# Keys and values of four attention heads as seven half-size products, in a two-layer hybrid decoder

## The chip, the cores and the metric

The program runs on one core of a Trainium2 chip. Its time is that of the device for one execution, in microseconds (us); where several runs are compared, their median stands. A core has five engines that take their own instructions in order and wait for each other by semaphores: TensorE (PE; its weight loads are listed as PEld), VectorE (DVE), ScalarE (ACT), GpSimd (POOL) and SyncE (SP). SP and POOL issue most of the DMA transfers.

## The reference

```python
DEPTH, SEQ, D_MODEL = 2, 512, 1024
def reference(x, ...):
    ...
    for l in range(DEPTH):
        x = x + 0.5 * swiglu(rms_norm(x, ffn1_norm[l]), ffn1_w_in[l], ffn1_w_out[l])
        h = rms_norm(x, mix_norm[l]) @ w_mix_in[l]
        (c_x, c_b, c_c, h_q, h_f, h_i, h_g, f_q, f_k, f_v, f_f) = jnp.split(h, split_at, axis=-1)
        y = jnp.concatenate([
            short_conv_mixer(c_x, c_b, c_c, conv_w[l]),
            hgrn2_mixer(h_q, h_f, h_i, h_g, lower_bounds[l], hgrn_out_gain[l]),
            fox_mixer(f_q, f_k, f_v, f_f, fox_f_bias[l], fox_q_gain[l], fox_k_gain[l]),
        ], axis=-1)
        x = x + y @ w_mix_out[l]
        x = x + 0.5 * swiglu(rms_norm(x, ffn2_norm[l]), ffn2_w_in[l], ffn2_w_out[l])
    return x
```

All of it is float32. The part called the mix has three token mixers side by side: a short convolution (256 channels), HGRN2, a gated linear recurrence in chunks of 64 tokens (4 heads of 64), and FoX, a forgetting attention (8 heads of 64, with normalised queries and keys). One matrix `w_mix_in` of 1024 rows makes the inputs of all three; f_q, f_k and f_v are 512 of its columns each.

## The kernel before

x stands transposed in SBUF, 1024 features in eight tiles of 128 by 512 tokens, times the gain of its norm, and as a pair of a rounded high part and the low rest. A float32 product is made of three matmuls: high by high, high by low, low by high (`mm3`, in the trace lines 328, 336 and 337).

Weights come in granules. `granule` (line 297) lets SP load a block into a buffer `st`, of which there are two; ScalarE casts it to its high part (line 314) and VectorE subtracts that from it for the low part (line 315), into a buffer `hl`, of which there are three. So a granule needs SP, then ScalarE, then VectorE before TensorE may use all of it.

The feed-forward networks on both sides of the mix already make their products in seven half-size products instead of eight (`plan`, `halved`, lines 783 to 827). There each operand is cut in half in both dimensions, and sums of weight blocks are made by DMA transfers that add to their target: line 786 adds from memory, line 827 from another tile.

In the mix the work is laid out so. First the inputs of HGRN2 are made (z, g, q with matmuls 512 wide, then v and the forget gates). Then `projections` gives Q, K and V of the first four FoX heads (`hf` 0) and then those of the second four (called Q', K', V' here). Each is a stream of four granules of two k-tiles by 256 columns, 24 matmuls of 128x256 per granule, one for each of four token tiles, two k-tiles and three parts. The four token tiles of one stream share two PSUM banks (three banks have the name `mm`, one `po`, two each `sc` and `pt`).

The generator `hgrn` makes the recurrence in ten parts, and between them takes a counted number of granules from `projections`: 2, 4, 4, 4 and so on, 23 steps in all. Its parts hold for each level of a chunk's triangle: on VectorE two sums T (lines 1435 and 1436 with their places), an exponential on ScalarE, a product `e` (line 1438), then on TensorE 64 small score matmuls (line 1352), and on VectorE predicated copies of the scores into A (lines 1446, 1455). The rest of `projections` is taken up while the attention of the first four heads begins (`fox_attend`), and the convolution's streams after it.

After Q and K (`fox_qkv`) come norms: ScalarE squares each bank (line 1555), VectorE reduces it (line 1556), small operations make 1/norm, and VectorE multiplies each bank into `qk` (line 1564). V is copied with its scale (lines 1572, 1573). The order in which each engine gets its instructions is set when the program is built, by priorities and the order of the code; on the chip every engine keeps that order.

Of the kernel before, what the change touches and what calls it, by code (L numbers as in the profile page):

```python
# [9 lines left out]
F32 = mybir.dt.float32  # L10
# [149 lines left out]
class Trunk:  # L160
# [875 lines left out]
    def mix(self, l, w, w_out, conv_w, out_gain, q_gain, k_gain, f_bias, next_gain):  # L1036
# [3 lines left out]
        with tc.tile_pool(name=self.n("mix"), bufs=1) as mp:  # L1040
# [3 lines left out]
            ]  # L1044
            self.yh = pair(mp, "cyh", F32R) + [None, None]
            self.yl = [None] * 4
            self.mp = mp
# [57 lines left out]
            for i in range(2):  # L1105
# [5 lines left out]
            ib = hp.tile([P, 4, P], F32, tag="t", name=self.n("ib"), bufs=self.tb)  # L1111
            self.invc, self.inv2 = col("invc", 4), col("inv2", 4)
            nc.vector.tensor_mul(
# [30 lines left out]
            def projections():  # L1144
                for hf in range(2):
                    yield from self.fox_qkv(mp, hf, tokens, half)
# [42 lines left out]

            def conv():  # L1190
                for i in range(2):
                    bx, bc = yield from features_steps(
                        [(C_X + i * P, P), (C_C + i * P, P)], ("mm", "mm")
                    )
# [347 lines left out]

    def fox_qkv(self, mp, hf, tokens, half):
        nc = self.nc
        qk = mp.tile([P, 4, 4, 2, HD], F32, tag="qk", name=self.n("qk"), bufs=2)
        for w, a in enumerate((F_Q, F_K)):
            banks = yield from tokens(a + 256 * hf, ("mm", "mm" if w == hf else "po"))
            s16 = lambda tag: mp.tile([P, 4, 4], F32, tag=tag, name=self.n(tag), bufs=2)
# [13 lines left out]
            for bi in range(2):  # L1562
# [3 lines left out]
                )  # L1566
        V = mp.tile([P, 4, 4, 2, HD], F32R, tag="V", name=self.n("V"), bufs=2)

        def copy(i, bank):
            src = bank[:, 256 * (i % 2) : 256 * (i % 2) + 256].rearrange("p (h d) -> p h d", d=HD)  # L1570
            sc = self.invc[:, i : i + 1]
            nc.scalar.activation(V[:, i, :, 0, :], src, AF.Copy, scale=sc)
            nc.vector.scalar_tensor_tensor(
                out=V[:, i, :, 1, :], in0=src, scalar=sc, in1=V[:, i, :, 0, :],
                op0=ALU.mult, op1=ALU.subtract,
            )

        banks = yield from tokens(F_V + 256 * hf, ("mm", "po" if hf else "mm"))
        for i in range(4):
            if hf and i > 1:  # L1580
                self.later.append(partial(copy, i, banks[1]))
            else:
                copy(i, banks[i // 2])
        half[hf] = qk, V
# [37 lines left out]
    def fox_attend(self, pool, hf, half, g, ops, made=None):  # L1622
# [24 lines left out]
        def values(h, i, PH, PL):  # L1647
# [3 lines left out]
            for j in range(i + 1):  # L1651
                u = 1 if j == i else 0
                for part in (PH, PL):
                    nc.tensor.matmul(  # L1654
                        self.ob[:, t0 + u * P : t0 + 2 * P],
                        V[:, j, h % 4].rearrange("p a d -> p (a d)"),
                        part[:, j, u:, :].rearrange("p i t -> p (i t)"),
# [265 lines left out]
```

## Time and profile before

| what | us |
|---|---|
| median of three runs | 1804.54 |
| lowest and highest | 1803.86, 1804.83 |
| the profiled execution | 1801.38 |
| span of its trace | 1799.6 |
| TensorE busy | 1792.0 |
| VectorE busy | 1430.1 |
| ScalarE busy | 1001.0 |
| GpSimd busy | 176.6 |

Busy times and the span are from the profiled execution, which took 3.16 us less than the median of the three runs. In the trace of layer 0, Q's last granule starts on TensorE at 394.88, K and V run from 397.72 to about 423.8 with scores of HGRN2 in between, and Q' follows. Layer 1 shows the same about 890 us later. The names behind an instruction are those of the program's tiles: `hl` a split granule, `st` its raw weights, `x` the low part of x, `mm` and `po` banks. A time of one instruction runs from its start to its end; where instructions follow each other without a gap, the distance of two starts is less, since they overlap a little.

### The profile page before, as it was taken

What the parts mean: (1) busy time and instruction counts of PE and PEld (TensorE: products, weight loads), DVE (VectorE), ACT (ScalarE), POOL (GpSimd) and SP (SyncE); (2) the same over time, 40 slices, a digit from 0 to 9 for tenths busy, and PEclk for the clock granted to TensorE, in tenths of its full rate; (3) what the DMA queues carried; (4) which work ended last, traced back from release to release, by engine and by line L of the source; (5) the groups of instructions that cost most, each with busy time, mean ns of one, the idle gap of its engine ahead of it and who ended that gap; (6) DMA issues with size and microseconds to landing.
All of it is one profiled execution on the core that took longest, in us unless ns stands there. A gap on an engine that the chain in (4) does not pass through costs nothing.

```text
span 1799.6 us, 34747 instructions
## 1 busy us (share of the span) xinstructions
PE 1792.0 (100%) x14271; PEld 1681.0 (93%) x14271; DVE 1430.1 (79%) x2006; ACT 1001.0 (56%) x1445; POOL 176.6 (10%) x184
## 2 busy tenths in 40 slices
PE   9999999999999999999999999999999999999999
PEld 7899999899888899999889999998998888999997
DVE  9889787676888798879679887876868879888793
ACT  5455554464776465556446555555547755555551
POOL 0011120100000002112001111201000000020210
PEclk9999999999999999999999999999999999999999
DMA  7659793233433857868265786913334346597762
GB/s 207 180 133 196 169 188 97 71 82 84 106 98 108 222 130 170 194 163 166 82 207 133 169 185 175 187 65 83 78 85 116 89 144 179 141 185 190 160 133 94
DMA packets 244638, 254.09 MB, mean 141 GB/s; under 512 B 18904, under 2 KB 228576, under 8 KB 244480
## 3 DMA queue, kind: packets, MB, share of 16 engines
q1 hardware_dynamic: 189424, 182.38, 33.7%
q0 software_dynamic: 54752, 69.23, 23.8%
q8 instruction: 112, 1.84, 0.4%
q14 instruction: 46, 0.38, 0.1%
q10 hardware_dynamic: 304, 0.27, 0.0%
HBM read 223.98 MB, written 2.10 MB: 126 GB/s over the span
## 4 chain that ended last, share of the span: by engine, by line
PE 94%; DVE 2%; ACT 2%; DMA 1%; issue 1%; SPq 0%; POOL 0%; ACTq 0%; DVEq 0%; POOLq 0%
PE mm L328 14%; PE mm L336 14%; PE mm L337 14%; PE sc L328 6%; PE sc L336 6%; PE sc L337 6%; PE pt L336 6%; PE pt L328 6%; PE pt L337 6%; PE po L328 4%; PE po L336 4%; PE po L337 4%; PE po L1654 1%; PE pt L1698 1%; PE pt L1352 1%
## 5 line engine op out<-in xcount | busy, mean ns | idle before, releaser
L810 ACT CAST hl<-w 128x1024 fp32r<-128x1024 f32 x322 | 336.8, 1050 | 305.9 <-PE mm L337 80.4
L812 DVE TENSOR_TENSOR hl<-w,hl 128x1024 fp32r<-128x1024 f32 x322 | 391.8, 1220 | 96.7 <-ACT hl L810 96.7
L315 DVE TENSOR_TENSOR hl<-st,hl 128x512 fp32r<-128x512 f32 (+3 forms) x196 | 162.5, 830 | 116.2 <-ACT hl L314 115.0
L314 ACT CAST hl<-st 128x512 fp32r<-128x512 f32 (+3 forms) x196 | 143.1, 732 | 174.3 <-PE po L337 66.8
L328 PE MATMUL mm<-xc,hl 128*128 128x256 f32 (+1 forms) x733 | 201.3, 276 | 0.0
L336 PE MATMUL mm<-xc,hl 128*128 128x256 f32 x728 | 201.2, 276 | 0.0
L337 PE MATMUL mm<-xc,hl 128*128 128x256 f32 x728 | 201.0, 276 | 0.0
L328 PE MATMUL sc<-xc,hl 128*128 128x256 f32 (+1 forms) x532 | 146.0, 276 | 0.0
L336 PE MATMUL sc<-xc,hl 128*128 128x256 f32 x528 | 146.0, 276 | 0.0
L337 PE MATMUL sc<-xc,hl 128*128 128x256 f32 x528 | 145.8, 276 | 0.0
L328 PEld LDWEIGHTS mm<-xc,hl 128*128 128x128 f32 x733 | 137.4, 188 | 0.2
L337 PEld LDWEIGHTS mm<-xc,hl 128*128 128x128 f32 x728 | 136.7, 188 | 0.0
L336 PEld LDWEIGHTS mm<-xc,hl 128*128 128x128 f32 x728 | 136.7, 188 | 0.0
L328 PE MATMUL pt<-xc,hl 128*128 128x256 f32 (+1 forms) x482 | 132.6, 276 | 0.0
L336 PE MATMUL pt<-xc,hl 128*128 128x256 f32 x480 | 132.6, 276 | 0.0
L337 PE MATMUL pt<-xc,hl 128*128 128x256 f32 x480 | 132.5, 276 | 0.0
L328 PE MATMUL mm<-x,hl 128*128 128x512 f32 x272 | 107.6, 396 | 0.0
L336 PE MATMUL mm<-x,hl 128*128 128x512 f32 x272 | 106.3, 391 | 0.0
L337 PE MATMUL mm<-x,hl 128*128 128x512 f32 x272 | 106.2, 390 | 0.0
L328 PEld LDWEIGHTS sc<-xc,hl 128*128 128x128 f32 x532 | 99.7, 188 | 0.2
L336 PEld LDWEIGHTS sc<-xc,hl 128*128 128x128 f32 x528 | 99.1, 188 | 0.0
L337 PEld LDWEIGHTS sc<-xc,hl 128*128 128x128 f32 x528 | 99.1, 188 | 0.0
(517 smaller groups left out, 5575.0 us busy)
## 6 DMA issues: line engine op xcount, KB each, us to landing
w<-in_ffn_w_in_dram SPq DMA_DIRECT2D x140, 512.0 KB, 5.1
w<-in_ffn_w_out_dram SPq DMA_DIRECT2D x64, 512.0 KB, 5.2
w<-in_ffn_w_out_dram POOLq DMA_DIRECT2D x56, 512.0 KB, 7.2
st<-in_w_mix_in_dram SPq DMA_DIRECT2D x88, 256.0 KB, 2.8
st<-in_ffn_w_in_dram SPq DMA_DIRECT2D x70, 256.0 KB, 3.1
w<-in_ffn_w_in_dram POOLq DMA_DIRECT2D x35, 512.0 KB, 8.9
w<-S POOLq DMA_DIRECT2D x35, 512.0 KB, 4.7
st<-in_ffn_w_out_dram SPq DMA_DIRECT2D x24, 512.0 KB, 5.3
```

The lines of the kernel that those rows point to most:

```text
L314: a = nc.scalar.copy(hi, src[:, c : c + w])
L315: b = nc.vector.tensor_sub(lo, src[:, c : c + w], hi)
L328: i = nc.tensor.matmul(acc[:, c], ah, bh[:, c], start=first and c.start == 0, stop=False, skip_group_check=True,)
L336: nc.tensor.matmul(acc, a, b, start=False, stop=False, skip_group_check=True)
L337: i = nc.tensor.matmul(acc, c, d, start=False, stop=last, skip_group_check=True)
L810: A(nc.scalar.copy(hi, src))
L812: return lambda: V(nc.vector.tensor_sub(lo, src, hi))
L1352: nc.tensor.matmul(bank[hh][rows[par], at + x * n : at + (x + 1) * n], held[rows[hh], c * CH : (c + 1) * CH], moving(rows[hh], c), start=T ...
L1654: nc.tensor.matmul(self.ob[:, t0 + u * P : t0 + 2 * P], V[:, j, h % 4].rearrange("p a d -> p (a d)"), part[:, j, u:, :].rearrange("p i t - ...
L1698: nc.tensor.transpose(tb[:, j * P : (j + 1) * P], p[:, j * P : (j + 1) * P], self.ident)
```

## The change

K and V of the first four heads are two blocks of 256 columns. With the columns of K and V as the two halves of one dimension, the 1024 rows of the weights cut into an upper and a lower 512, and the 512 tokens cut into two halves of 256, the product consists of eight half-size products of 24 matmuls each. The change makes them from seven, P1 to P7, with Winograd's sums: four combinations of x and four of the weights.

- `fox_sums` makes the combinations of x: sixteen scaled copies on ScalarE, four subtractions on VectorE, then a high part (ScalarE) and a low part (VectorE) of each. Its steps stand beside the first parts of `hgrn`.
- `fox_halved` takes the place of the streams of K and V. Weights come as blocks of 512 KB (line 1608 of the new file) instead of 256 KB. Four weight sums are made by DMA on POOL's queue (line 1611): P5's block plus another from memory, P6's plus P5's, P3's plus P6's, P7's plus another from memory. Each product's block is split in 128x1024.
- Results are put together in PSUM and with three bank copies (ScalarE) and two additions (VectorE). V comes out negated and is copied with a negated scale.
- `projections` counts seven steps for K and V where it counted eight; the counts taken by `hgrn` are the same.
- Buffers: the raw blocks of P5 and P7 share one tile with the convolution's high part, the other sums use tags of tiles that are used later (`V0` to `V3`, `qk`, `cyl`, `hy`).

```diff
 def mix(...):
+            nc.scalar.activation(self.ninvc, self.invc, AF.Copy, scale=-1.0)
...
+            sums = self.fox_sums(mp)
+            next(sums)
             dense = projections()
...
+                if part:
+                    next(sums, None)
...
+    def fox_sums(self, mp):
...
+                    nc.scalar.activation(
+                        f[a, b][:, k, :], self.xT[:, j, b * H : (b + 1) * H], AF.Copy,
+                        scale=self.gain[:, j : j + 1],
+                    )
...
+        def part(name, at, hi, lows):
+            nc.scalar.copy(hi, f[at])
+            n = 4 // len(lows)
+            for i, lo in enumerate(lows):
+                ks = slice(n * i, n * i + n)
+                nc.vector.tensor_sub(lo, f[at][:, ks, :], hi[:, ks, :])
...
+        nc.vector.tensor_sub(f[0, 0], f[0, 0], f[0, 1])
+        part("P5", (0, 0), high[:, 0], [
...
+        yield
+        nc.vector.tensor_sub(f[0, 1], f[1, 1], f[0, 1])
+        negative((1, 1), (0, 0))
+        negative((1, 0), (1, 1))
+        part("P6", (1, 1), high[:, 1], [four("V0", F32R)])
+        yield
+        part("P7", (0, 1), more[:, 0], [four("V3", F32R)])
+        part("P4", (1, 0), more[:, 1], [four("V1", F32R)])
...
+    def fox_halved(self, mp, w, cols):
...
+            nc.sync.dma_start(t, src(q))
...
+        add = lambda x, y: nc.gpsimd.dma_start(x, y, accum_op=ALU.add)
...
+            if p in ("P5", "P7"):
+                add(raws[p], src(3 if p == "P5" else 0))
+            elif p in ("P6", "P3"):
+                add(raws[p], raws["P5" if p == "P6" else "P6"])
+
+        c, a, b = (self.bank(t) for t in ("mm", "mm", "po"))
+        bank = {"P1": a, "P2": c, "P5": b, "P6": a, "P3": b, "P7": a, "P4": a}
...
+        order = ("P1", "P2", "P5", "P6", "P3", "P7", "P4")
+        for p in order[:3]:
+            load(p)
+        for n, p in enumerate(order):
+            with self.tc.high_priority():
+                hi, lo = self.parted(raws[p].rearrange("p k c -> p (k c)"), 1, SKEW_MOVING)
...
+            if n + 3 < len(order):
+                load(order[n + 3])
...
+            if p == "P1":
+                nc.scalar.copy(c, a)
+            elif p == "P5":
...
+                nc.scalar.copy(tmp[1], b)
+            elif p == "P6":
+                nc.scalar.copy(tmp[0], a)
+            elif p == "P3":
+                nc.vector.tensor_add(tmp[0], tmp[0], b)
+                done = (c, tmp[0])
+            elif p == "P7":
+                nc.vector.tensor_add(tmp[1], tmp[1], a)
+            yield done if p == "P3" else None
+        return (a, tmp[1])
```

The change alters the order on the engines. On VectorE, in layer 0, this stands before from the scan S of HGRN2's state on, where TensorE makes K (hl are the low parts of K's granules, `fm` Q's norm, T and `e` the levels of HGRN2):

```order
L1389 SCALAR_TENSOR_TENSOR S_4334<-T_4333,T_4332 128x1024
L1556 TENSOR_REDUCE fm_4371<-qk_4132 128x8
L315 TENSOR_TENSOR hl_4450<-st_4448,hl_4450 128x512
L1556 TENSOR_REDUCE fm_4371<-qk_4132 128x8
L1436 TENSOR_TENSOR T_4481<-b_4107 128x256x2
L1557 TENSOR_TENSOR fm_4371<-fm_4371,inv_446_3891 128x16
L1435 TENSOR_TENSOR T_4693<-kb_4108,b_4107 128x128x4
L1436 TENSOR_TENSOR T_4693<-b_4107 128x128x4
L1438 TENSOR_TENSOR e_526_4482<-T_4481,q_3880 128x512
L315 TENSOR_TENSOR hl_4557<-st_4555,hl_4557 128x512
```

And so it stands now from the same scan on; hl_4493, hl_4610 and hl_4640 are the low parts of P5, P6 and P3, xs_4604 and xs_4607 those of the combinations of x for P7 and P4:

```order
L1395 SCALAR_TENSOR_TENSOR S_4362<-T_4361,T_4360 128x1024
L1682 TENSOR_REDUCE fm_4405<-qk_4154 128x8
L1442 TENSOR_TENSOR T_4530<-b_4129 128x256x2
L1572 TENSOR_TENSOR xs_4604<-xs_4099,xh_4103 128x1024
L315 TENSOR_TENSOR hl_4493<-st_4429,hl_4493 128x1024
L1682 TENSOR_REDUCE fm_4405<-qk_4154 128x8
L1444 TENSOR_TENSOR e_540_4531<-T_4530,q_3878 128x512
L315 TENSOR_TENSOR hl_4610<-st_4435,hl_4610 128x1024
L1683 TENSOR_TENSOR fm_4405<-fm_4405,inv_444_3889 128x16
L1572 TENSOR_TENSOR xs_4607<-xs_4100,xh_4103 128x1024
L1441 TENSOR_TENSOR T_4742<-kb_4130,b_4129 128x128x4
L315 TENSOR_TENSOR hl_4640<-st_4466,hl_4640 128x1024
```

The low parts are twice as wide, and two of x stand among them. Further on, behind Q's norm and the predicated copies, VectorE now has this up to the product `e` of the third level (hl_4685 and hl_4713 belong to P7 and P4):

```order
L1690 TENSOR_TENSOR qk_4154<-mm_4156,fr_4406 128x8x64
L1442 TENSOR_TENSOR T_4742<-b_4129 128x128x4
L1441 TENSOR_TENSOR T_4748<-kb_4130,b_4129 128x64x8
L315 TENSOR_TENSOR hl_4685<-st_4496,hl_4685 128x1024
L1444 TENSOR_TENSOR e_554_4743<-T_4742,q_3878 128x512
L1442 TENSOR_TENSOR T_4748<-b_4129 128x64x8
L1441 TENSOR_TENSOR T_4953<-kb_4130,b_4129 128x32x16
L315 TENSOR_TENSOR hl_4713<-st_4613,hl_4713 128x1024
L1682 TENSOR_REDUCE fm_4668<-qk_4154 128x8
L1444 TENSOR_TENSOR e_556_4749<-T_4748,q_3878 128x512
```

Before, the third `e` stood directly behind Q's norm, ahead of the predicated copies; now two wide low parts and the work of two levels stand between.

On TensorE, P6 is now followed by one matmul of Q' and the first scores that read that third `e`, ahead of P7 (the rows show where a wait stands; P7 is the row with hl_4685):

```order
L337 MATMUL mm_4423<-hl_4610,xs_4373 128x256
L328 MATMUL mm_4833<-hl_4837,x_379_3549 128x256 [waits DVE_49,Activation_49]
L1358 MATMUL sc_4740<-e_556_4749,T_4748 64x32 [waits DVE_49]
...
L1358 MATMUL sc_4740<-e_556_4749,T_4748 64x32
L328 MATMUL mm_4423<-hl_4685,xh_4103 128x256 [waits Activation_49]
L336 MATMUL mm_4423<-hl_4685,xh_4103 128x256
```

Before, these scores stood between V's third and fourth granule. The whole order of the products on TensorE is now P1, P5, scores of level 2, P3, P2, P6, the rows above, P7, more scores, P4, the rest of the scores, Q'.

On POOL these four sums are new in each layer; a row of small work lies between the first two:

```order
L1611 DMA st_4429<-in_w_mix_in_dram 128x4x256 [waits DMAHW2_49,DMASW6_49]
L1407 MEMSET lf_4526 128x2x64 [waits DVE_49,Activation_49]
L1611 DMA st_4435<-st_4429 128x1024 [waits DMAHW3_49,DMAHW4_49,DMAHW2_49,DMAHW5_49,DMAHW0_49,DMAHW6_49,DMASW7_49,DMAHW7_49,DMASW6_49,DVE_49]
L1611 DMA st_4466<-st_4435 128x1024 [waits DMAHW3_49,DMAHW1_49,DMAHW5_49,DMASW7_49,DMAHW7_49,DMASW0_49,DVE_49]
L1611 DMA st_4496<-in_w_mix_in_dram 128x4x256 [waits DMAHW2_49,DMASW1_49,DVE_49]
```

On SP eight loads of K and V by 256 KB have given way to seven of 512 KB; st_4429, the raw block of P5, is loaded while the first inputs of HGRN2 are made, and st_4496, that of P7, takes the same place in SBUF later.

More of the change, by code (lines that the diff above doesn't have):

```diff
@@ L1044, in mix @@
             ]
-            self.yh = pair(mp, "cyh", F32R) + [None, None]
-            self.yl = [None] * 4
+            self.yh, self.yl = [None] * 4, [None] * 4
             self.mp = mp
@@ L1111, in mix @@
             ib = hp.tile([P, 4, P], F32, tag="t", name=self.n("ib"), bufs=self.tb)
-            self.invc, self.inv2 = col("invc", 4), col("inv2", 4)
+            self.invc, self.inv2, self.ninvc = col("invc", 4), col("inv2", 4), col("ninvc", 4)
             nc.vector.tensor_mul(
@@ L1145, in projections @@
                 for hf in range(2):
-                    yield from self.fox_qkv(mp, hf, tokens, half)
+                    yield from self.fox_qkv(mp, hf, tokens, half, w)
+            sums = self.fox_sums(mp)
+            next(sums)
             dense = projections()
@@ L1190, in conv @@
             def conv():
+                hi = mp.tile([P, 2, T], F32R, tag="cyh", name=self.n("cyh"))
                 for i in range(2):
+                    self.yh[i] = hi[:, i, :]
                     bx, bc = yield from features_steps(
@@ L1544, in fox_qkv, with normed @@
+    def fox_qkv(self, mp, hf, tokens, half, w_in):
         nc = self.nc
         qk = mp.tile([P, 4, 4, 2, HD], F32, tag="qk", name=self.n("qk"), bufs=2)
-        for w, a in enumerate((F_Q, F_K)):
-            banks = yield from tokens(a + 256 * hf, ("mm", "mm" if w == hf else "po"))
+        V = None
+        def normed(w, banks):
             s16 = lambda tag: mp.tile([P, 4, 4], F32, tag=tag, name=self.n(tag), bufs=2)
```

97 lines of the change are left out of this document (87 added, 10 removed).

## The prediction

> **What bounds the kernel now.** I read the busy table and the chain of waits first, then the list of who waits for whom, then busy time by stage, then the instructions one by one in the stretch that the change touches.
>
> ```profile
> span 1799.6 us, 34747 instructions
> PE 1792.0 (100%) x14271; PEld 1681.0 (93%) x14271; DVE 1430.1 (79%) x2006; ACT 1001.0 (56%) x1445; POOL 176.6 (10%) x184
> PE 94%; DVE 2%; ACT 2%; DMA 1%; issue 1%; SPq 0%; POOL 0%; ACTq 0%; DVEq 0%; POOLq 0%
> ```
>
> TensorE is busy for 1792.0 of 1799.6 us, and 94% of the chain that ended last is TensorE. The list of waits (engine, line, who was waited for; total, times, longest) begins so:
>
> ```profile
> PE pt L1698 <- DVE QA L1600: 1.3, 2, 0.6
> PE mm L1815 <- DVE z L1802: 1.2, 1, 1.2
> ```
>
> The longest wait of TensorE is 1.2 us. So any matmul that goes shortens the program, provided the others still find their operands ready; and any wait that the change makes is paid in full. The question is how much room the other engines have where the products stand. By stage (columns as in the header):
>
> ```profile
> core 0: us, PE busy (x) PEld busy (x) DVE busy (x) ACT busy (x) POOL busy (x), PEclk, DMA share, GB/s
> 345.00:382.00 37.00, 37.00 (x210) 32.63 (x209) 27.86 (x40) 20.54 (x28) 2.98 (x5) 1.00 0.38 92
> 395.00:417.50 22.50, 22.50 (x308) 22.36 (x309) 22.17 (x39) 12.59 (x22) 0.00 (x0) 1.00 0.28 72
> 417.50:450.00 32.50, 32.50 (x542) 31.97 (x541) 17.39 (x39) 12.91 (x29) 0.00 (x0) 1.00 0.32 83
> 1285.00:1310.00 25.00, 25.00 (x395) 24.73 (x395) 23.88 (x45) 13.62 (x26) 0.00 (x0) 1.00 0.30 76
> ```
>
> From 395.0 to 417.5, where K and V are made in layer 0, VectorE is busy 22.17 of 22.50 us (layer 1, from 1285 on: 23.88 of 25.00). TensorE does not wait there, since VectorE has begun early; but VectorE has no free time left. That row decides the forecast.
>
> **The change part by part, for one layer.**
>
> *Removed: 24 matmuls.* Eight groups of 24 become seven. In TensorE's timeline of before, K's first three granules run thus:
>
> ```profile
> 394.88 0.39 PE L328 MATMUL mm<-hl,x 128*128 128x256 f32 x1
> 397.72 0.28 PE L328 MATMUL mm<-hl,x 128*128 128x256 f32 x1
> 405.77 0.28 PE L337 MATMUL po<-hl,x 128*128 128x256 f32 x1
> 405.97 1.14 PE L1352 MATMUL pt<-e,T 64*64 64x32 f32 x64
> 407.94 0.39 PE L328 MATMUL mm<-hl,x 128*128 128x256 f32 x1
> ```
>
> From 397.72 to 405.77 lie 71 steps, 8.05 / 71 = 0.1134 us each. 24 of them are 2.72 us, so 5.44 us over both layers. That is the whole gain. The scores in between (128 small matmuls of L1352, of which the row shows half) took 407.94 - 405.97 = 1.97 us.
>
> *Added on VectorE: subtractions of double width.* A step of this engine is the distance between starts:
>
> ```profile
> 386.12 1.22 DVE L1361 TENSOR_TENSOR T<-q,k 128x1024 f32<-128x1024 f32 x1
> 387.26 0.68 DVE L315 TENSOR_TENSOR hl<-st,hl 128x512 fp32r<-128x512 f32 x1
> ...
> 395.00 1.28 DVE L1394 TENSOR_TENSOR A<-ident,pt 128x512 f32<-128x512 f32 x2 [0.64 <-PE pt L1352]
> 396.20 0.69 DVE L1435 TENSOR_TENSOR T<-kb,b 128x512 f32<-128x512 f32 x1
> 396.80 2.29 DVE L1389 TENSOR_TENSOR_SCAN S<-T,T 128x1024 f32<-128x1024 f32 x1
> 399.00 0.66 DVE L1556 TENSOR_REDUCE fm<-qk 128x8 f32<-128x512 f32 x1
> 399.58 0.68 DVE L315 TENSOR_TENSOR hl<-st,hl 128x512 fp32r<-128x512 f32 x1
> ...
> 406.98 1.29 DVE L1564 TENSOR_TENSOR qk<-mm,fr 128x512 f32<-128x512 f32 x2
> ...
> 408.79 0.68 DVE L1438 TENSOR_TENSOR e<-T,q 128x512 f32<-128x512 f32 x1
> 409.39 1.31 DVE L1446 COPY_PREDICATED A<-lmask,pt 128x256 f32<-128x256 uint8 x2
> 410.49 1.39 DVE L1455 COPY_PREDICATED A<-lmask,pt 128x256 f32<-128x256 uint8 x2
> 411.66 0.73 DVE L1435 TENSOR_TENSOR T<-kb,b 128x512 f32<-128x512 f32 x1
> ```
>
> So 128x1024 costs 387.26 - 386.12 = 1.14 us, 128x512 0.60 (396.20 to 396.80), the scan 2.20, the reduction 0.58, the four predicated copies 411.66 - 409.39 = 2.27. Both versions of the queue are gated at the same place: A waits for the sums of L1352 that end just before Q's fourth granule (395.00 before). From there I add up the changed queue in its written order, which this engine keeps, up to the third `e`, on which TensorE's scores of level 3 wait (the row `e_556` of the order):
>
> - up to P5's low: A twice 1.20, T 0.60, scan 2.20, reduction 0.58, T 0.60, the low of P7's combination 1.14, P5's low 1.14: 7.46, at 402.5.
> - up to P3's low: reduction 0.58, e 0.60, P6's low 1.14, a small one 0.08, the low of P4's combination 1.14, T 0.60, P3's low 1.14: 5.28, at 407.7.
> - Q's norm and the predicated copies: 2.27, two of qk 1.20, five small ones about 0.4: 3.9, at 411.6.
> - to the third e: T 0.60, T 0.65, P7's low 1.14, e 0.60, T 0.60, T 0.65, P4's low 1.14, reduction 0.58, e 0.69: 6.65, at 418.3.
>
> Together 23.3 us, against 14.4 before (395.00 to the end of the third e, 408.79 + 0.6). Seven lows of 1.14 us are in it, two of them for combinations of x that before does not have.
>
> TensorE has less to do in the same stretch. From 394.9 to that place stand Q's fourth granule, P1, P5, the scores of level 2, P3, P2, P6, and one matmul of Q' (the Q of the second four heads): six groups of 2.72, 1.97 and 0.11, together 18.4 us, at 413.3. It needs the third e, which is there at 418.3. **TensorE must lose 418.3 - 413.3 = 5.0 us per layer**, wherever the waits fall. By my times they fall so: P5 waits for its low (TensorE is through with P1 at 400.4, the low at 402.5: 2.2); P3 for its low (about 0.5); P2 for the copy of P1's bank, which comes behind Q's norm in its other bank (about 1.5); the scores for e (the rest, 0.8). The range of this term: every step could be 0.03 shorter or the queue start 0.3 sooner, 4.3; the steps as the busy means say (0.68 and 1.22) would give 8 and more, but the rows of start to start exclude that; I keep 4.3 to 5.6.
>
> *Added by DMA: four sums of weights on POOL's queue.* Nothing of this kind stands in the mix of before; the nearest rows are those of the FFN (the DMA of L827 adds one tile in SBUF to another, L786 adds from memory, L783 is a plain load of 512 KB by SP):
>
> ```profile
> L827 POOL DMA_DIRECT2D w<-S x35: 877/887/897, 73.2 to 1729.6; - x35
> DMA to landing us min/median/max: 4.5/4.7/6.4
> ...
> L786 POOL DMA_DIRECT2D w<-in_ffn_w_in_dram x35: 1283/1425/1669, 38.8 to 1711.9; - x35
> ...
> DMA to landing us min/median/max: 5.6/7.8/14.0
> ...
> L783 SPq DMA_DIRECT2D w<-in_ffn_w_in_dram x124: 367/368/1652, 56.8 to 1716.4; - x124
> ...
> DMA to landing us min/median/max: 3.4/5.0/12.6
> ```
>
> P5's sum is loaded long ahead. P6's raw block is loaded by SP when P1's buffer is free (about 392.3): 3.9 us, then two adds in SBUF behind each other on POOL (P5 to P6, P6 to P3), 4.6 each: 405.4. With the cast of 1.05 P3's block is ready at 406.5, and VectorE comes to it at 406.6: just in time, worth 0 to 1. P7's raw block goes into P5's buffer, so SP may issue it only at 402.5, behind P5's low (SP's loads of P4 and of Q' are queued behind it). It lands after 3.4 to 5.0; POOL then adds from memory in 5.6 to 7.8: 411.5 to 415.3; with the cast VectorE may take it at 412.6 to 416.4. Its place in the queue is at 412.8. So VectorE, and TensorE with it, loses a further 0 to 3.6 us. The stretch has a DMA share of 0.28, the FFN's stage below 0.91, so the smallest values are nearer: I take **1.2**.
>
> ```profile
> 135.00:180.00 45.00, 45.00 (x400) 45.00 (x399) 40.57 (x42) 23.27 (x27) 8.60 (x7) 1.00 0.91 196
> ```
>
> The Trainium skill ("DMA: Bandwidth & Descriptors", section "Anatomy of one DMA — SWDGE (gpsimd) path") gives 2.0 us plus the bytes over 436 KB per us, an estimate of 3.2 us for 512 KB. The row of L827 shows 4.7 for such a transfer with an add, so the trace does not bear the page out for adds; by the page P7 would never be late and this term would be nothing.
>
> *Added on ScalarE and VectorE ahead of it: the sums of x.* Sixteen scaled copies of 128x256, four casts and the four combinations, with P5's and P6's lows, stand in the 37 us before 382: VectorE gains 2 x 1.14, 2 x 1.15 and 2.3, about 6.9 us, against 37.00 - 27.86 = 9.1 idle; ScalarE gains sixteen of about 0.4 and two or three casts of 1.05, about 9, against 16.5 idle. I cost it at nothing; its cover are the 210 long matmuls there. If the combinations came in front of T (kd) on VectorE, that product would be late for the transposes at 384.9; following the queue I have it at 381.4. Bounds 0 and 1.5.
>
> *Copies and evacuations.* Three bank copies on ScalarE (0.60 each by the row of L1555 below) and two more additions of 0.60 on VectorE replace nothing on TensorE but the waits above; P4 waits for the addition of P7's bank for about 0.1.
>
> ```profile
> 396.56 0.60 ACT L1555 ACTIVATE qk<-mm 128x512 f32<-128x512 f32 x1 [0.29 <-PE mm L337]
> 397.92 0.62 ACT L314 CAST hl<-st 128x512 fp32r<-128x512 f32 x1 [0.76 <-PE mm L337]
> ```
>
> *Moved: one granule less beside the attention.* The 23 counted steps now reach one granule further into Q', K' and V', so one group of 2.72 us less is left to fill the front of the attention. Before has 17.39 of 32.50 us of VectorE there and TensorE is full; I take 0.3, bounds 0 and 1.5. Everything from the convolution's products on stands in the same order in both.
>
> Sum per layer: -2.72 + 5.0 + 1.2 + 0.1 + 0.3 = +3.9; both layers **+7.8 us**. The profiled execution of before took 1801.38 us; that gives 1809.2 for one like it. The median of the runs is 1804.54, so the forecast is 1804.54 + 7.8 = 1812.3, rounded to **1812**: slower.
>
> **The rivals.**
>
> *The cover holds (faster).* VectorE's lead carries the wider lows as it carries the narrow ones now, and the 48 matmuls are gained: 1804.54 - 5.44 = 1799.1. For it: before, VectorE is full as well and TensorE waits nowhere; in the FFN TensorE takes 400 such matmuls in 45.00 us with VectorE 40.57 busy, row above, and those are half products with lows of 128x1024. Against it: there 0.90 of VectorE is enough; here it has 23.3 us of work to TensorE's 18.4. It would need the stretch to take less than 18.4, or the third e to be needed later than the order says. Decided at the point where P5 starts: before 400.8 the rival holds, at 402 or later it falls.
>
> *It comes out even.* The gate at 395 moves up or the queue's steps overlap better, and the stretch is near 20.8 us, so that a loss of 2.4 to 2.7 per layer meets the gain: about 1804.5. Against it: each step used is start to start from a queue that was full.
>
> *The adds by DMA are the bound (slower still).* At the FFN's medians P7 is ready at 402.5 + 5.0 + 7.8 + 1.05 = 416.4, 3.6 us behind its place; with P6's load at 5.0 and adds of 4.7, P3's block is ready at 392.3 + 5.0 + 9.4 + 1.05 = 407.8, 1.2 late, which pushes all behind it. The loss is then about 8.4 instead of 6.2 per layer: 1804.54 + 2 x (-2.72 + 5.0 + 3.6 + 0.4) = about 1817. For it: both median rows. Against it: the low DMA share of the stretch.
>
> The clock is granted in full in every window above, 1.00. The Trainium skill ("TensorE: Matmul & The Clock Gate", section "Part 1: The HAM clock gate (the "warmup" mystery)") says that it halves after an idle window of about 3.4 us; no wait in before is that long, so no run here shows it yet, and by that rule only the last rival, with one wait beyond that length, would cost more.
>
> **How the numbers follow.** Forecast as summed, 0.50; adds as the bound, 0.17; even, 0.18; the cover holds, 0.15. A measurement of this kernel can tell about 0.2% (3.6 us) from no change: faster is below 1800.9, slower above 1808.1. Even holds some cases that are just slower or just faster, and the forecast's low end (4.3 per layer, P7 in time: +3.6) just touches 1808. Faster 0.15, same 0.19, slower 0.66. The forecast's own range is 1808 to 1816. The range for 8 in 10 takes in the rival of the adds and most of the even cases: 1801 to 1818.
>
> **What would show it.** K and V of the first four heads should show 168 matmuls per layer instead of 192. Right: TensorE's waits list has new lines for P5 (po, line 336, waiting for VectorE's low of L315), for P2 (mm, line 328, waiting for ScalarE's copy of P1's bank) and for the scores in front of P7, about 2, 1.5 and 1 us and twice each; the window from 395 shows TensorE near 0.8 busy and VectorE near 1.0. P7's add should land 5.6 to 7 us after its issue, behind a load issued at the end of P5's low. Wrong: if TensorE stays at 100% between 395 and 420, the queue was not the bound and the time is near 1799; if VectorE itself has holes before P7's low, the adds are the cause and the time is above 1814; and if the waits appear before 385 or after 430, I have costed the sums of x or the attention's front at too little.

## The result

The changed kernel takes 1828.61 us (median of four runs, 1826.58 to 1830.10); the kernel before took 1804.2 us beside it. The ratio is 1.0138, 95% interval 1.0120 to 1.0155; the medians lie 24.4 us apart. Slower was forecast, but at 1812 us with a range up to 1818. VectorE's queue, the largest term of the forecast's sum, is there to 0.3 us per layer; the terms beside it were under-priced.

The page of the changed kernel, first lines and the chain of waits by engine:

```profile
span 1824.8 us, 34720 instructions
PE 1799.5 (99%) x14223; PEld 1684.4 (92%) x14223; DVE 1454.6 (80%) x2026; ACT 1030.5 (56%) x1491; POOL 185.8 (10%) x192
PE 88%; DVE 4%; DMA 3%; ACT 3%; issue 1%; POOL 0%; ACTq 0%; SPq 0%; POOLq 0%; DVEq 0%
```

TensorE has 48 matmuls fewer, worth 5.4 us, and yet is busy for 1799.5 us, 7.5 more than before. "Busy" does not mean work done here: some matmuls took longer. DMA has 3% of the chain in place of 1%. The list of TensorE's waits now begins so (total, times, longest):

```profile
PE po L336 <- DVE hl L315: 4.0, 2, 2.1
PE mm L328 <- ACT hl L314: 3.4, 2, 2.6
PE pt L1358 <- issue: 2.7, 1, 2.7
PE sc L1358 <- DVE e L1444: 1.7, 2, 0.9
PE po L328 <- ACT ks L1657: 1.6, 1, 1.6
PE mm L328 <- DVE q L1125: 1.4, 2, 1.1
PE sc L1777 <- DVE nm L1782: 1.4, 2, 0.7
PE sc L1777 <- DVE KB L1762: 1.4, 2, 0.7
```

The first line is P5's wait for its low, 1.90 us in layer 0 and 2.08 in layer 1 (forecast: 2.2). The second is the wait of the one matmul of Q' for its cast (0.71 and 2.65 us), which on ScalarE stands behind P7's late cast. "issue" in the third means that the profile shows nothing that TensorE waited for. VectorE's timeline of layer 0 shows what else happened. The first row is A, where the forecast's sum began, the last is the third `e`, on which the scores wait:

```profile
396.54 1.28 DVE L1400 TENSOR_TENSOR A<-ident,pt 128x512 f32<-128x512 f32 x2
...
407.54 0.68 DVE L1441 TENSOR_TENSOR T<-kb,b 128x512 f32<-128x512 f32 x1
411.02 1.23 DVE L315 TENSOR_TENSOR hl<-st,hl 128x1024 fp32r<-128x1024 f32 x1 [2.80 <-ACT hl L314]
...
416.34 0.68 DVE L1441 TENSOR_TENSOR T<-kb,b 128x512 f32<-128x512 f32 x1
419.46 1.23 DVE L315 TENSOR_TENSOR hl<-st,hl 128x1024 fp32r<-128x1024 f32 x1 [2.44 <-ACT hl L314]
...
424.14 0.68 DVE L1444 TENSOR_TENSOR e<-T,q 128x512 f32<-128x512 f32 x1
```

From A to the end of that `e` are 424.82 - 396.54 = 28.28 us. Two holes stand in it, 2.80 ahead of P3's low and 2.44 ahead of P7's; without them 23.04 us of work remain, where the forecast summed 23.3. In layer 1 it is 28.53 with holes of 1.85 and 3.64, so 23.04 again. ScalarE's timeline names what the casts ahead of these lows waited for:

```profile
409.94 1.04 ACT L314 CAST hl<-st 128x1024 fp32r<-128x1024 f32 x1 [2.87 <-DMA st<-st]
418.38 1.05 ACT L314 CAST hl<-st 128x1024 fp32r<-128x1024 f32 x1 [2.54 <-DMA st<-in_w_mix_in_dram]
```

Both are adding transfers: the first is P3's sum, tile to tile, the second P7's, from memory. POOL's timeline shows the chain (and the wait ahead of each issue):

```profile
398.29 0.91 POOL L1611 DMA_DIRECT2D st<-st  x1 [7.39 <-DMA st<-in_w_mix_in_dram]
403.50 0.85 POOL L1611 DMA_DIRECT2D st<-st  x1 [4.30 <-DVE xs L1572]
411.42 1.30 POOL L1611 DMA_DIRECT2D st<-in_w_mix_in_dram  x1 [7.07 <-DMA st<-in_w_mix_in_dram]
```

P6's raw block, which SP issued at 393.84, was there at about 398.2, 2 us later than I had it; 1.5 of these are the lateness of the whole stretch (the row of A below). The first add landed after 4.57 us (402.86), as the FFN's rows said. The second took 6.37 (403.50 to 409.87), with P7's raw load beside it from 404.10 (in layer 1, with the same load beside it from 1304.76, 5.49); and that load in turn needed some 7 us, until 411.3, before P7's own add could start, which took 6.86. The Trainium skill ("DMA: Bandwidth & Descriptors", section "Anatomy of one DMA — SWDGE (gpsimd) path") would give an estimate of 3.2 us for each; 4.5 was the least that the trace of this kernel shows.

And TensorE's clock fell, which no window of before showed. By stretch, the first three of layer 0, the rest of layer 1:

```profile
408.00:412.00 4.00, 1.30 (x79) 1.22 (x72) 1.20 (x2) 1.63 (x3) 0.58 (x1) 0.79 0.57 160
412.00:417.50 5.50, 5.50 (x28) 5.49 (x28) 5.03 (x13) 0.57 (x1) 0.73 (x1) 0.53 1.02 206
417.50:423.00 5.50, 5.50 (x48) 5.34 (x46) 3.54 (x5) 4.50 (x5) 0.00 (x0) 1.00 0.04 6
...
1311.30:1316.20 4.90, 4.72 (x26) 4.43 (x27) 4.90 (x13) 0.57 (x1) 1.30 (x1) 0.65 0.96 215
...
1326.50:1332.20 5.70, 5.70 (x42) 5.42 (x41) 2.97 (x6) 1.64 (x3) 0.00 (x0) 0.53 0.22 64
```

The ninth number, without the counts in brackets, is the granted clock. P3 in layer 0, the first part of P3 in layer 1, and P7 in layer 1 ran at half clock: TensorE is "busy" for 5.50 us of 412.0 to 417.5 and gets 28 matmuls done, where it makes 48 in the next 5.5. P3's 24 matmuls took 5.2 us (412.09 to 417.27) in place of 2.7. The waits ahead of these were 2.70, 1.56 and 2.65 us long.

Set side by side by the start of the same event in both timelines (in us; the third mark is TensorE's first score on the third `e`, for before the place where the same count of work is done, A + 18.3; the fourth is the first `sc<-A,v`, before which both kernels have done the same number of matmuls):

| mark | layer 0 before, after | late by | layer 1 before, after | late by |
|---|---|---|---|---|
| norm of the mix | 345.39, 346.35 | 0.96 | 1235.64, 1246.22 | 10.58 |
| A on VectorE | 395.00, 396.54 | 1.54 | 1284.87, 1297.20 | 12.33 |
| scores on the third e | 413.3, 424.88 | 11.6 | 1303.2, 1325.79 | 22.6 |
| `sc<-A,v` | 450.37, 462.59 | 12.22 | 1340.24, 1366.15 | 25.91 |
| norm of the second FFN | 594.44, 605.05 | 10.61 | 1483.66, 1508.67 | 25.01 |

The first 0.96 us arise in the first 8 us of the program, where nothing was changed. Layer 0 then costs 9.65 us and layer 1 14.43, against 3.9 forecast for each.

### The profile page after: what moved, and what is told of

It reads as the page before. It is cut to its first block, busy times and chain, and to the rows that moved or that the text cites. A ratio compares the mean times of both kernels' runs of the same rounds, so it can differ in the third digit from the quotient of the medians.

```text
span 1824.8 us, 34720 instructions
## 1 busy us (share of the span) xinstructions
PE 1799.5 (99%) x14223; PEld 1684.4 (92%) x14223; DVE 1454.6 (80%) x2026; ACT 1030.5 (56%) x1491; POOL 185.8 (10%) x192
## 4 chain that ended last, share of the span: by engine, by line
PE 88%; DVE 4%; DMA 3%; ACT 3%; issue 1%; POOL 0%; ACTq 0%; SPq 0%; POOLq 0%; DVEq 0%
PE mm L328 12%; PE mm L337 12%; PE mm L336 12%; PE sc L328 6%; PE sc L336 6%; PE sc L337 6%; PE pt L328 6%; PE pt L336 6%; PE pt L337 6%; PE po L337 3%; PE po L336 3%; PE po L328 3%; DMA st<-in_w_mix_in_dram 2%; DVE hl L315 1%; PE po L1800 1%
## 5 line engine op out<-in xcount | busy, mean ns | idle before, releaser
L315 DVE TENSOR_TENSOR hl<-st,hl 128x512 fp32r<-128x512 f32 (+3 forms) x194 | 168.6, 870 | 116.1 <-ACT hl L314 115.3
L314 ACT CAST hl<-st 128x512 fp32r<-128x512 f32 (+3 forms) x194 | 148.0, 765 | 166.6 <-PE po L337 53.9
```

The source lines that it names most:

```text
L314: a = nc.scalar.copy(hi, src[:, c : c + w])
L315: b = nc.vector.tensor_sub(lo, src[:, c : c + w], hi)
```

## The experiments

Theory A: the adding transfers come late, TensorE waits for what they deliver, and in those waits its clock falls. Theory B: VectorE's queue alone makes the loss, and the adds would be in time otherwise. In all runs the ratio is against the kernel before, measured beside them.

**Without the adds.** The four adding transfers are left out.

```diff
-            if p in ("P5", "P7"):
-                add(raws[p], src(3 if p == "P5" else 0))
-            elif p in ("P6", "P3"):
-                add(raws[p], raws["P5" if p == "P6" else "P6"])
```

> The four transfers that add weight blocks are left out; each product takes its first raw block alone, so K and V are not the reference's. All else, the order on VectorE and TensorE too, stays. Theory A (the adds are late and the clock falls in the waits that they make): VectorE's holes of 1.9 to 3.6 us ahead of P3's and P7's low vanish, the queue's loss of 5.0 us per layer stays, the clock is 1.00 throughout, about 1814 us. Theory B (VectorE's queue alone makes the loss, and the adds would be in time if it were shorter): no change, 1826 to 1829 us.

Measured: 1815.91 us, ratio 1.0073 (1.0058 to 1.0088), 12.7 us less than the changed kernel (11.7 by the two ratios, since the kernel before took 1802.41 us beside this run). A's number was 1814. From A to the end of the third `e` VectorE now needs 24.70 and 24.67 us: P7's hole is gone, P3's has shrunk to 1.5 us and has another cause:

```profile
406.92 1.05 ACT L314 CAST hl<-st 128x1024 fp32r<-128x1024 f32 x1 [1.55 <-PE po L337]
```

P3's cast waits for TensorE to leave P5's split buffer (there are three), and P5 ran at half clock in this run, in both layers: the window from 402.0 has a clock of 0.55, though the wait ahead was 2.09 us long and P5 at the same place of the changed kernel, after waits of 1.90 and 2.08 us, ran at 1.00.

```profile
402.00:405.30 3.30, 2.88 (x13) 2.88 (x14) 3.30 (x6) 0.57 (x3) 0.00 (x0) 0.55 0.51 143
```

So the adds account for about half of the 24.4 us, and the claim that the clock would be 1.00 throughout failed.

**The lows of x earlier.** Two of VectorE's seven wide lows move ahead of A.

```diff
         part("P6", (1, 1), high[:, 1], [four("V0", F32R)])
-        yield
         part("P7", (0, 1), more[:, 0], [four("V3", F32R)])
         part("P4", (1, 0), more[:, 1], [four("V1", F32R)])
```

> The splits of x's combinations for P7 and P4 are emitted one step earlier, with that for P6, so two lows of 1.14 us leave VectorE's queue behind the scan. Theory A: the adds set the time, so only what comes ahead of P5's low counts, 1.1 us per layer, about 1826 us, with longer holes ahead of P3's and P7's low. Theory B: 2.3 us per layer or more, 1824 us or less, and the holes stay as they were.

Measured: 1825.91 us, ratio 1.0130 (1.0115 to 1.0145); A's number. VectorE's work from A to the third `e` falls from 23.04 to 18.57 us. That is four lows of 1.14 us, not two: with the two of x gone from the stretch, the lows of P7's and P4's weights now come behind the third `e` (P7's at 424.42, when that `e` has ended at 422.44), so three of seven are left. But what VectorE gains it waits: one hole of 4.96 and 4.70 us ahead of P3's low, with ScalarE idle for 6.15 us:

```profile
413.57 1.04 ACT L314 CAST hl<-st 128x1024 fp32r<-128x1024 f32 x1 [6.15 <-DMA st<-st]
```

**Both.** No adds and the earlier lows.

> Both: no adds (K and V not the reference's) and the two splits earlier. Theory A: 2.3 us per layer below the run without adds alone, about 1809 us. Theory B: as the run with early splits alone, about 1824 us.

Measured: 1811.86 us, ratio 1.0051 (1.0036 to 1.0066). The two edits give 4.0 us more together than the first alone, where A had 4.6 and, starting from 1814, a time of 1809; B's 1824 is out. VectorE has no hole between A and the third `e`, 18.5 us in both layers with three wide lows, so the queue is now as long as TensorE's own 18.3, and P5 waits 0.95 us in place of about 2. The clock is 1.00 over the whole run. A new wait of 1.35 and 0.98 us stands earlier, for the cast `flh` of the forget gates: in front of its input VectorE now has the two moved lows.

**The sums of x alone.** K and V again as eight streams; the combinations are made and not used.

```diff
-            if w and hf == 0:
-                steps = self.fox_halved(mp, w_in, (F_K, F_V))
...
+            banks = yield from tokens(a + 256 * hf, ("mm", "mm" if w == hf else "po"))
+            normed(w, banks)
```

> The seven products are undone (K and V again as eight streamed granules each of half width), the combinations of x are still made but not used. It prices them alone. If they are hidden as I predicted, 1804 to 1806 us. If they are part of the loss (TensorE waited 0.3 and 1.1 us for the evacuation of q in the two layers of the changed kernel), 1807 us or more, with these waits in both layers.

Measured: 1802.57 us, ratio 1.0002 (0.9992 to 1.0011): hidden, as forecast. In the window where they are made VectorE is busy 34.09 us of 37 (27.86 before), ScalarE 27.83 (20.54), TensorE all of it:

```profile
345.00:382.00 37.00, 37.00 (x210) 32.57 (x209) 34.09 (x47) 27.83 (x46) 2.98 (x5) 1.00 0.40 94
```

The waits for q of the changed kernel (0.33 and 1.10 us) are not there, so they don't belong to the sums alone.

**P6's block in a place of its own.** The whole change with its adds, the lows of x earlier, and P6's raw block in the buffer that P4's combination has left.

```diff
-                "cyh" if p in ("P5", "P7") else "st",
+                {"P5": "cyh", "P7": "cyh", "P6": "V2"}.get(p, "st"),
```

> The whole change with all its adds, the two splits of x earlier (as in the second run), and P6's raw block in the buffer that P4's combination of x leaves free (V2), so that its load and its add don't wait for P1's buffer and P3's add can run some 6 us sooner. Theory A (late adds): P3's and P7's holes on VectorE go, and the time is that of the run without adds and with early splits, 1812 us, up to 1816 if P7's add is still a little late. Theory B' (the adds cost by their traffic on the DMA engines, not by when they start): 1820 us or more.

Measured: 1812.74 us, ratio 1.0058 (1.0041 to 1.0075). All transfers are there, the same bytes, and the time is that of the run without any of them (1811.86). The adds start at 391.78 and 400.19 in place of 398.29 and 403.50, and VectorE has no hole between A and the third `e`: 18.51 us in both layers. Only P7's low, which stands behind that `e` here, still waits, 0.76 and 0.44 us. The run with the lows of x earlier differs from this one by the place of P6's block alone and took 1825.91 us: 13.2 us more, with the same transfers. So what the adds cost was when they started, not what they moved. The time is still 10.7 us above the kernel before.

```profile
391.78 0.91 POOL L1610 DMA_DIRECT2D st<-st  x1 [41.14 <-ACT negc L1543]
...
400.19 0.85 POOL L1610 DMA_DIRECT2D st<-st  x1 [7.29 <-issue]
408.96 1.30 POOL L1610 DMA_DIRECT2D st<-in_w_mix_in_dram  x1 [7.92 <-DVE ft L432]
```

**Other offsets for the weights, and plain x.** In the changed kernel a matmul of P5, P6, P7 and P4 steps by 0.120 us in place of 0.113. Two runs looked for the reason, both on the kernel without adds and with early lows.

```diff
-                hi, lo = self.parted(raws[p].rearrange("p k c -> p (k c)"), 1, SKEW_MOVING)
+                hi, lo = self.parted(raws[p].rearrange("p k c -> p (k c)"), 1, {"P6": 16, "P7": 0, "P4": 32}.get(p, SKEW_MOVING))
```

> As the run without adds and with early splits (K and V not the reference's), but the split weights of P6, P7 and P4 stand at other offsets in their buffer: 16, 0 and 32 elements in place of 48 (P5 keeps 48). If the 0.120 us that a matmul of these products takes (0.1134 with plain x) come from where weights and combinations of x lie relative to each other in SBUF, some of the three go at 0.1134 and the time falls by up to 1.5 us; if they come from something else, all four stay at 0.120 and the time at 1812 us.

```diff
-                        ah, al = self.mixed[p](k, t)
+                        ah, al = (z[k][:, t] for z in (self.xh, self.xl))
```

> As the run without adds and with early splits, but P5, P6, P7 and P4 read plain tiles of x in place of the combinations, which are made and left unused (K and V are not the reference's). If the 0.120 us of their matmuls come from the tiles in which the combinations lie, the steps fall to 0.1134 and the time by 1.3 us, to about 1810.5 us. If they come from the weights' side, they stay at 0.120 and the time at 1812 us.

Measured: 1812.37 and 1812.87 us. The median step was 0.1195 (P5, 48 elements), 0.117 (P6, 16), 0.1195 (P7, 0) and 0.117 (P4, 32), so the offset is worth at most 0.003 us. With plain x P5 went at 0.114, but from 413 us on every product went at 0.118, Q' too, which takes 0.113 in the kernel before. In the changed kernel itself the plain matmuls of Q and P1 step by 0.118 in layer 0 and by 0.113 in layer 1, so the combinations alone don't make the step either. What sets it between 0.113 and 0.120 stays open. It is worth about 0.6 us per layer (96 matmuls by 0.0065).

**One granule more for the attention's front.**

```diff
         yield 1
         yield 0
-        yield 2
+        yield 1
```

> As the run without adds and with early splits, but the recurrence takes one granule less (22 steps), so that the front of the attention has as many granules beside it as before the change. If the granule missing there makes the two new waits of 0.7 us at the first scores (1.1 us per layer with all), they go and the time falls by about 2 us, to 1810 us. If the granule is missed as much at the recurrence's end, 1812 us.

Measured: 1811.48 us, ratio 1.0051 (1.0036 to 1.0066), the same as without the edit (1811.86). The first of the two waits at the first scores grew from 0.7 to 1.1 us, the other stayed at 0.7. So the granule missing as cover is not what makes them. They wait for VectorE (`KB` and `nm` in the list above), which comes to these rows late; why was not followed further.

**P5's wait filled with work.** As the run without adds, P1 made twice.

```diff
-            for i in range(2):
+            for i in (0, 1, 0, 1) if p == "P1" else (0, 1):
```

> As the run without adds, but P1's 24 matmuls are made twice, the first set overwritten by the second: 2.7 us more of TensorE work just where it waits 2.1 us for P5's low. If the half clock in P5 (0.55 and 0.67 granted in the run without adds) comes from that wait, P5 runs at 1.00 and a layer costs 0.6 us more and 2.3 less: about 1812 us. If the clock falls for another reason, P5 stays at half and the time is 1816 us or, with the 2.7 us in full, up to 1821.

Measured: 1816.52 us, ratio 1.0080 (1.0065 to 1.0095). P5 ran at full clock in both layers, where it had run at half in both layers with the wait. But the time did not fall, since the scheduler moved other work as well and P3 now waited 0.93 and 0.75 us. After these two waits the clock fell in layer 0 and not in layer 1, with the same work and the same waits on both sides. The trace shows what differs. In every run the granted clock changes only at steps of 3.413 us: here it was 0.50 from 411.28 to 414.69, and in the changed kernel from 410.31 to 417.14 (two steps) and next from 1311.42 on, 894.28 us or 262 steps after that. Counted on in these steps, both waits of layer 0 (407.94 to 408.87, 409.26 to 410.01) lie in one step, the one that ended when the clock fell. In layer 1 a border at 1305.57 goes through the first wait (1304.93 to 1305.86):

```profile
407.86:411.28 3.42, 1.74 (x19) 1.46 (x12) 3.42 (x7) 1.53 (x3) 0.00 (x0) 1.00 0.63 165
411.28:414.69 3.41, 3.41 (x18) 3.41 (x17) 3.41 (x7) 0.63 (x1) 0.00 (x0) 0.50 0.22 70
...
1302.15:1305.57 3.42, 2.78 (x135) 2.56 (x133) 3.42 (x8) 2.66 (x4) 0.00 (x0) 1.00 0.17 56
1305.57:1308.98 3.41, 2.37 (x18) 2.17 (x19) 3.41 (x6) 0.81 (x2) 0.00 (x0) 1.00 0.76 214
1308.98:1312.39 3.41, 3.41 (x31) 3.41 (x31) 3.41 (x7) 1.31 (x2) 0.00 (x0) 1.00 0.04 14
```

**Decay first, and lows on GpSimd.** Both on the kernel with P6's block in its own place; the second has the edit of the first too.

```diff
                 if part < 2:
-                    next(decay, None)
+                    with tc.high_priority():
+                        next(decay, None)
```

> As the run with P6's raw block in its own place (all adds, result as the reference), but the operations of the forget gates' decay get priority on ScalarE and VectorE over the splits of P7's and P4's x, which there stand ahead of the cast flh, so that TensorE waits 1.34 us for it in both layers. If that wait is a cost of its own, it goes, and the time falls by 2 to 2.7 us, to about 1810 us. If VectorE's queue behind it takes back what it gives, 1812.7 us.

Measured: 1818.40 us, ratio 1.0091 (1.0074 to 1.0107), worse than the 1812.74 that it started from. The wait for `flh` did not go but grew to 1.97 us in both layers: VectorE still has the two lows of x (384.30, 2.48 us) ahead of the forget gates' first addition (387.30). The expectation had put the wait on ScalarE's order; it is VectorE's. This wait's growth, 1.2 us over both layers, is not the whole 5.7 us; TensorE's list has 0.8 us more for a copy of `v` and 0.6 for `q` too, and the rest was not followed.

```diff
-            b = nc.vector.tensor_sub(lo, src[:, c : c + w], hi)
+            b = (low or nc.vector).tensor_sub(lo, src[:, c : c + w], hi)
...
+                ..., low=nc.gpsimd if p in ("P6", "P4") else None)
```

> As the run before in this call, but the low parts of P6's and P4's weights are made on GpSimd in place of VectorE, so that two steps of 1.14 us leave VectorE's queue per layer. If VectorE's queue is still what TensorE waits for, 1 to 2.3 us less per layer, 1806 to 1808 us. If GpSimd needs more than about 4 us for one (no run shows such an operation yet) or holds up the adds that stand behind it in its queue, P6 and P7 wait for it and the time is 1812 us or more.

Measured: 1824.33 us, ratio 1.0120 (1.0105 to 1.0135), 5.9 us above the kernel with decay first from which it differs by this edit alone. One subtraction of 128x1024 took GpSimd about 2.46 us, not the 4 us beyond which I expected a loss; yet VectorE won nothing. GpSimd's timeline and VectorE's beside it, in layer 0:

```profile
405.21 2.49 POOL L315 TENSOR_TENSOR hl<-st,hl 128x1024 fp32r<-128x1024 f32 x1 [4.72 <-ACT hl L314]
```

```profile
405.35 2.39 DVE L1683 TENSOR_TENSOR fm<-fm,inv 128x16 f32<-128x16 f32 x1
407.66 0.68 DVE L1442 TENSOR_TENSOR T<-kb,b 128x512 f32<-128x512 f32 x1
...
423.66 0.69 DVE L1661 TENSOR_TENSOR ks<-ks,po 128x512 f32<-128x512 f32 x1 [1.39 <-ACT ks L1659]
424.26 1.93 DVE L315 TENSOR_TENSOR hl<-st,hl 128x512 fp32r<-128x512 f32 x1
```

An operation of VectorE on 128x16, 0.17 us elsewhere, lasted 2.39 us, just as long as GpSimd's subtraction beside it; layer 1 shows the same (2.40 beside 2.51). VectorE stood still meanwhile, and its work from A to the third `e` stayed at 18.4 us, though P6's low had left it. Beside P4's low on GpSimd (423.23 to 425.65) it was not quite still: an addition that reads a PSUM bank, `ks<-ks,po`, took its usual 0.69 us, and only the subtraction behind it, with both inputs in SBUF, was held for 1.93 us in place of 0.68. The Trainium skill ("SBUF — State Buffer", section "Terms", on the "shared port pair" of VectorE and GpSimd) says that the loser blocks for the whole instruction; the 2.39 and 1.93 us of these rows agree. P3 then waited 1.13 us in layer 0 and 2.23 in layer 1, and the clock after it was 0.50 and 0.52.

No version with the seven products came near the kernel before. Even with the adds early, 10.7 us remain, so some 16 us are lost against 5.4 saved. The list of TensorE's waits in that version (P6's block in its own place) names 9.7 us of them, none of which the kernel before has:

```profile
PE sc L1538 <- ACT flh L1532: 2.7, 2, 1.3
PE mm L328 <- ACT ks L1658: 2.1, 2, 1.2
PE po L336 <- DVE hl L315: 2.1, 3, 1.0
PE sc L1776 <- DVE nm L1781: 1.4, 2, 0.7
PE sc L1776 <- DVE KB L1761: 1.4, 2, 0.7
```

How many of these come from splits of twice the width was not isolated.

## Why the prediction was wrong

The sign and the first mechanism, VectorE's longer queue, were right; the size was not: 24.4 us in place of 7.8. The step that failed is the price of the adds, 1.2 us per layer, and with it the clock, which the sum put at nothing. By the terms of the sum, per layer, from the table of marks:

| term | forecast | layer 0 | layer 1 | from |
|---|---|---|---|---|
| VectorE's queue | 5.0 | 4.7 | 4.7 | 23.04 of work less TensorE's 18.3 |
| adds late | 1.2 | 5.2 | 5.5 | the holes, 2.80 + 2.44 and 1.85 + 3.64 |
| from the third e to `sc<-A,v` | 0.1 | 0.6 | 3.3 | 12.22 - 11.6, 25.91 - 22.6 |
| ahead of A | 0 | 0.6 | 1.75 | 1.54 - 0.96, 12.33 - 10.58 |
| matmuls saved, and the attention's front | -2.4 | -1.6 | -0.9 | 10.61 - 12.22, 25.01 - 25.91 |
| sum | 3.9 | 9.5 | 14.4 | |

**The queue** held: 23.04 us measured in both layers, 23.3 summed, and with three wide lows in place of seven it is 18.5, the same sum less four times 1.14. What the term costs in the program's time is less sure: without adds, taking these four lows out gave 4.0 us in all, not 4.7 per layer, since other waits grew. Adding up an in-order queue from steps start to start was sound.

**The adds are the term that failed.** The step read "the stretch has a DMA share of 0.28, the FFN's stage below 0.91, so the smallest values are nearer". The share of 0.28 was that of the kernel before. The change itself puts six loads of 512 KB and three adds between 385 and 418, and the share became 0.97 from 398 to 402 and 0.93 from 411 to 418:

```profile
398.00:402.00 4.00, 4.00 (x36) 4.00 (x35) 4.00 (x5) 3.99 (x6) 0.91 (x1) 1.00 0.97 238
...
411.00:418.00 7.00, 6.21 (x33) 6.19 (x34) 6.00 (x13) 1.15 (x3) 1.30 (x1) 0.56 0.93 190
```

So the FFN's medians (4.7, 5.0 and 7.8) were the nearer prices, and worse was to come for P3's add (6.37) and P7's load (about 7), as these two ran at the same time. The rival "the adds by DMA are the bound" was what happened, and its sign, holes on VectorE ahead of P7's low and a time above 1814, is in the trace. It too was priced too low: its sum counts 3.6 us for the adds, with P3's 1.2 inside P7's (its loss is then 8.6 per layer; the text's 8.4 is a slip), where both holes came in full, 5.2 and 5.5. The chance given to it, 0.17, rested on that same share. Two runs showed it: without the adds P7's hole went and P3's shrank, and 12.7 us with them; with P6's block in a place of its own the holes went and 13.2 us with them.

**The clock** is what that rival lacked. The text let it fall only after one wait beyond 3.4 us, the rule of the Trainium skill ("TensorE: Matmul & The Clock Gate", section "Part 1: The HAM clock gate (the "warmup" mystery)"). Here it fell to half after single waits of 1.56, 1.90, 2.09 and 2.65 us, for 3.41 or 6.83 us at a time; the idle time that the Trainium skill gives did not hold as a safe bound, though its half did (0.50). Not all of it lies on the path: in layer 0 P3's half clock cost nothing of its own, since P7's block came later still and TensorE waited again, 0.71 and 0.74 us, ahead of the scores on the third `e`; in layer 1 P7's 24 matmuls took 5.4 us in place of 2.85, which is most of the 3.3 in the table. In the run with P1 made twice, where P5's wait is filled, P5's half clock went in both layers, which ties the fall to the wait.

**The sums of x** were hidden, 1802.57 against 1802.41. The 0.6 and 1.75 us ahead of A in the changed kernel, with the wait for q among them, thus come from the rest of the change; which part was not isolated.

**The attention's front** cost 1.1 and 1.8 us, in and above the bounds of 0 to 1.5, where I took 0.3. The reason given, a granule less as cover, fell: putting it back changed nothing.

Of the waits that would show each step, P5's was right to 0.3 us. P2's was hidden behind P3's slow clock in layer 0; without the adds it shows, 0.75 and 0.65 us where 1.5 was forecast. The price of a slower step of the new products (0.6 us per layer) was not foreseen at all.

## What to carry to other kernels

Price a transfer at the load that the change will make there, not at the load that the trace of before shows; and where one buffer lets a chain of load, add and split start only when another split is done, write down the whole chain with two of its transfers running at once. An in-order queue of a full engine can be summed to a per cent from start-to-start steps, so a wide operation added to it is a loss that can be known beforehand. And once TensorE waits at all, two microseconds of waiting can cost as much again in clock.

## What was not expected of the hardware

The granted clock fell to 0.50 during or just after waits of 1.56, 1.90, 2.09, 2.65 and 2.70 us and after 0.93 and 0.75 us close together, and did not fall after waits of 1.90 and 2.08 us ahead of P5 in the changed kernel, or after 0.93 and 0.75 in the other layer of the same run. Its changes lie on a grid of 3.413 us in every trace, so a phase of low clock lasted 3.41 or 6.83 us, and where a wait lies on that grid counts. How much idle time within one step is enough is not settled: 1.90 us were in layer 1 of the run without the adds, 1.89 us were not in layer 1 of the changed kernel, and the step of the changed kernel that ended in the fall at 410.31 held only 1.2 us of waiting, with 2 us of the small score matmuls ahead of it.

Transfers of 512 KB that add tile to tile took 4.5 to 4.6 us in the changed kernel and, with a plain load of the same size starting 0.6 to 0.7 us after them, 5.49 and 6.37; that load itself took about 7 in layer 0. GpSimd subtracted 128x1024 float32 in 2.46 us, about twice VectorE's 1.14, and in that time VectorE did not advance with work whose inputs are both in SBUF (0.17 us became 2.39), while an addition that reads a PSUM bank took its usual 0.69.
